# A decoder layer on one core: x and the first weights in one array, two warming products, a last tile of 512, 320 and 192 columns

## The chip, the core and the metric

The kernel runs on one core of a Trainium2 chip. A core has a matrix engine (TensorE, PE in the profile; its weight loads are a row of their own, PEld), a vector engine (VectorE, DVE), an activation engine (ScalarE, ACT), a general engine (GpSimd, POOL) and an engine that only issues transfers (SyncE, SP). Each engine works through its own queue in the order of the program and waits on semaphores for the others. SP and ACT issue the transfers (DMAs) between the chip's main memory and the core's on-chip memory SBUF; products are summed in a second one, PSUM, which the kernel uses as eight banks of 512 fp32 columns.

The metric is the time of one execution on the device in microseconds (us), as the median of several executions.

## What is computed

One layer of a decoder with two parallel mixers over 512 tokens of width 1024, and a gated feed-forward block, all in fp32:

```python
proj = x @ w_in[layer]                     # q, k, v, the SSM's input u (512 columns), gate logits
u = proj[..., 3 * QKV_WIDTH:3 * QKV_WIDTH + SSM_WIDTH]
...
mix_out = mixed.astype(x.dtype) @ w_out[layer]
h = layer_norm(DN_ALPHA * x + mix_out.astype(x.dtype), ln1_g[layer], ln1_b[layer])
ff = (jax.nn.silu(h @ w_ff_gate[layer]) * (h @ w_ff_up[layer])) @ w_ff_down[layer]
x = layer_norm(DN_ALPHA * h + ff.astype(h.dtype), ln2_g[layer], ln2_b[layer])
```

Between the lines shown lie dilated attention in three groups, a state-space model (SSM) on u, and the gates. The change touches how the first product, u, gets its operands, and how the last normalization is reached.

## The kernel before

**Splitting.** The kernel gives TensorE its operands in a rounded form of fp32 (fp32r). To keep fp32 accuracy each operand is split into a high part, which ACT makes with a copy (L181), and a low part, the difference, which DVE makes (L182). Each product is then three: high by high, high by low, low by high (`mm3`, L188 to L190). The cast and the difference of any operand must be done before its products.

**The start.** The first product is u. `xT`, x transposed, lies in main memory as 128 partitions by eight k-slices of 512 tokens; the weights of u lie in two units of four k-slices of 512 columns each. SBUF receives x in tiles big4 and big5 (k 0 to 3, k 4 to 7) and the weights in big0 and big1. The slice k = 0 comes in two halves of 256 columns: SP issues the two of x (L276), ACT the two of the weights (L262). Then DVE clears a small tile `warm` (L263), ACT runs one exponential (L264), and TensorE runs three products of the cleared tile, 384 columns wide and in full fp32 (L267), which serve no result. ACT also issues `small`, 24 KB of SSM parameters (L280). SP goes on with x and weights in turn (L271, L258): k = 1, 2 and 3 singly, then 4 and 5, then 6 and 7, each of x and of the weights on its own, and then the streamed weight units (`raw`, L118) and small constants.

The splits of k = 0 (L479, L480, L321) go by halves: for each half ACT casts x, ACT or DVE casts the weights, DVE makes both differences. The other slices are split whole. Between the slices DVE runs some operations on 128 by 16 tiles from `small` (the queue called late, L78): four after k = 0 and k = 1, ten after each later k.

`u_tiles` (L595) does the products: for k = 0 the first two of four row blocks in two halves of 256 columns, then the other two blocks with 512, then for each k four blocks by three products of 512 columns. Its sums are copied out, and the products of the first v (`pv`) follow; these read x in another order of tokens, from tiles `xt` that ACT copies (L495). The first of them lies in big4 again, the second in big5.

**The end.** The feed-forward block's last product (`down`) sums 22 k-slices for four token tiles t of 128 rows and two halves of 512 columns. Its last four k-slices (NLAST) are done tile by tile, so that the normalization of a tile runs beside the products of the next. A tile's normalization is: DVE adds h to each half and measures it (`bn_stats`, L1267), combines the records (`bn_aggr`, L1268), adds the epsilon (L313); POOL takes the power −1/2 (L1100). `normalize_shared` then spreads the rest: DVE does the first half in two steps (both show as L318); for the second half DVE makes a small operand nm (L318, 128 by 1), ACT scales (L1125), POOL multiplies and adds (L1126, L1127). SP stores both halves (L1232).

The last tile, t = 3, has its sum of the first k-slices and h added early. Its last four k-slices are done in four pieces of 256 columns (`last_quarter`: 12 products, an add L321, a measurement L1259). The first piece is issued inside tile 2's `normalize_shared`, between its first step and nm, so on DVE's queue the order is: first step of tile 2, add and measurement of the piece, nm, second step of tile 2, then the pieces 1 to 3, the combination (L1276), L313, and both halves of the last tile in two steps each. POOL's queue has tile 2's L1126 and L1127 and then the last tile's power. SP and ACT store 64 rows each.

Of the kernel before, what the change touches and what calls it, by code (L numbers as in the profile page):

```python
# [10 lines left out]
F32 = mybir.dt.float32  # L11
# [3 lines left out]
ALU = mybir.AluOpType  # L15

P = 128
S = 512
D = 1024
KT = D // P  # L20
NTT = S // P
# [132 lines left out]
def emit(ctx, tc, i, out):  # L154
# [9 lines left out]
    def bank(n, name):  # L164
        return ps.tile([P, 512], F32, tag=f"b{n}", name=name)
# [13 lines left out]
    def split(hi, lo, src, scale=None):  # L179
        if scale is None:  # L180
            act.copy(hi, src)  # L181
            dve.tensor_tensor(lo, src, hi.bitcast(F32), op=ALU.subtract)  # L182
# [31 lines left out]
    def big(n, name, dt=F32):  # L214
        return pa.tile([P, 2048], dt, tag=f"big{n}", name=name)
# [30 lines left out]

    warm = at.tile([P, 512], F32, tag="un", name="warm", bufs=4)
    wact = sa.tile([P, 1], F32, name="wact")
    xr = [big(4 + j, f"x_raw{j}") for j in range(2)]
    xp = act_pair("x")  # L250
    wu = [big(j, f"wu_raw{j}").rearrange("p (k c) -> p k c", k=4) for j in range(2)]
    wup = [[home(j, f"wu{n}{j}", F32R).rearrange("p (k c) -> p k c", k=4) for j in js] for n, js in (("h", (3, 6)), ("l", (7, "g3")))]
    small = sa.tile([P, 3, NGP], F32, name="small")

    cols256 = [slice(0, 256), slice(256, 512)]

    def load_u(k0, k1, queue):
        queue.dma_start(wu[k0 // 4][:, k0 % 4 : k0 % 4 + k1 - k0],  # L258
                        i["w_in"][k0 // 4].rearrange("p (k c) -> p k c", k=4)[:, k0 % 4 : k0 % 4 + k1 - k0])

    for e in cols256:
        act.dma_start(wu[0][:, 0, e], i["w_in"][0][:, e])  # L262
    dve.memset(warm[:, 0:P], 0.0)  # L263
    act.activation(wact, warm[:, 0:1], AF.Exp)  # L264
    wb_ = dense("warm_b")
    for _ in range(3):
        pe.matmul(wb_[:, 0:384].rearrange("p (n m) -> p n m", n=3), warm[:, 0:P], warm[:, 0:P].unsqueeze(1).broadcast_to([P, 3, P]),  # L267
                  start=True, stop=True)

    def load_x(k0, k1):  # L270
        sp.dma_start(xr[k0 // 4][:, 512 * (k0 % 4) : 512 * (k0 % 4 + k1 - k0)], i["xT"][:, 512 * k0 : 512 * k1])  # L271

    for k0, k1 in ((0, 1), (1, 2), (2, 3), (3, 4), (4, 6), (6, 8)):
        if k0 == 0:
            for e in cols256:
                sp.dma_start(xr[0][:, e], i["xT"][:, e])  # L276
        else:
            load_x(k0, k1)
        if k0 == 0:
            act.dma_start(small, i["ssm_small"])  # L280
        else:
            load_u(k0, k1, sp)
    w.n_dma = 2
    w.n_split = 4
    w.load()
# [34 lines left out]
    def tt(o, a, b, op, eng=dve):  # L320
        eng.tensor_tensor(o, a, b, op=op)  # L321
# [145 lines left out]
            ts(neg[:, n], z, -1.0, ALU.mult, eng=eng)  # L467


    def split_x(k):  # L470
        split(xp[0][k // 4][:, k % 4, :], xp[1][k // 4][:, k % 4, :], xr[k // 4][:, 512 * (k % 4) : 512 * (k % 4) + 512])

    for k in range(KT):
        if k == 0:

            (xh, uh), (xl, ul) = ((z[0][:, 0, :] for z in (xp[n], wup[n])) for n in range(2))
            xs, us = xr[0][:, 0:512], wu[0][:, 0, :]
            for n, c in enumerate(cols256):
                act.copy(xh[:, c], xs[:, c])  # L479
                (act.copy if n else dve.tensor_copy)(uh[:, c], us[:, c])  # L480
                tt(xl[:, c], xs[:, c], xh[:, c].bitcast(F32), ALU.subtract)
                tt(ul[:, c], us[:, c], uh[:, c].bitcast(F32), ALU.subtract)
            late.take(4)
            continue
        split_x(k)
        split(wup[0][k // 4][:, k % 4], wup[1][k // 4][:, k % 4], wu[k // 4][:, k % 4])
        late.take(4 if k < 2 else 10)


# [626 lines left out]
    def normalize_shared(z, mv, ln, between=None):  # L1116

        nm = bt.tile([P, 1], F32, tag="nm", name="nm")
        lo, hi = halves
        norm_first(z, mv, ln, lo)  # L1120
        if between:
            between()
        stt(nm, mv[:, 0:1], -1.0, mv[:, 3:4], ALU.mult, ALU.mult)
        norm_second(z, mv, ln, lo)
        act.activation(z[:, hi], z[:, hi], AF.Identity, bias=nm, scale=mv[:, 3:4])  # L1125
        pool.tensor_tensor(z[:, hi], z[:, hi], ln[:, 0, hi], op=ALU.mult)  # L1126
        pool.tensor_tensor(z[:, hi], z[:, hi], ln[:, 1, hi], op=ALU.add)  # L1127
# [122 lines left out]
    bsts = [bt.tile([P, 4, 6], F32, name=f"bstb{t}", bufs=1) for t in range(NTT)]  # L1250
    mvs = [bt.tile([P, 4], F32, name=f"mvb{t}", bufs=1) for t in range(NTT)]
    quarters = [slice(256 * q, 256 * q + 256) for q in range(4)]

    def last_quarter(q):
        b = bank(4 + q, f"dq{q}")[:, 0:256]
        for k in range(NFF - NLAST, NFF):
            down(b, k, NTT - 1, quarters[q], k == NFF - NLAST, k == NFF - 1)
        tt(end[:, quarters[q]], end[:, quarters[q]], b, ALU.add)
        dve.bn_stats(bsts[NTT - 1][:, q, :], end[:, quarters[q]])  # L1259

    for t in range(NTT - 1):
        z, bst, mv = hn[t], bsts[t], mvs[t]
        for e, cs in enumerate(halves):
            for k in range(NFF - NLAST, NFF):
                down(acc[t][e], k, t, cs, False, k == NFF - 1)
            stt(z[:, cs], z[:, cs], ALPHA, acc[t][e], ALU.mult, ALU.add)
            dve.bn_stats(bst[:, e, :], z[:, cs])  # L1267
        dve.bn_aggr(mv[:, 0:2], bst[:, 0:2])  # L1268
        rstd(mv)
        normalize_shared(z, mv, lnb2, (lambda: last_quarter(0)) if t == NTT - 2 else None)  # L1270
        for cs in halves:
            store((sp, sp), t, z, cs)
    for q in range(1, 4):
        last_quarter(q)
    mv = mvs[NTT - 1]
    dve.bn_aggr(mv[:, 0:2], bsts[NTT - 1])  # L1276
    rstd(mv)
# [29 lines left out]
def layout(a):  # L1307
# [37 lines left out]
    return {  # L1345
        "x": x, "xT": xT, "w_in": np.concatenate(parts), "w_br": np.concatenate([units(a[n][0], 4, 256).reshape(2, 2, P, 1024).transpose(0, 2, 1, 3).reshape(2, P, 2048)
                                for n in ("w_ssm_br", "w_attn_br")]),
        "w_glu": pairs(glu.reshape(512, 1024), 4, 256), "w_out": units(a["w_out"][0], 4, 512)[[0, 2, 1, 3]],
        "w_gu": pairs(gu, 8, P), "w_dn": units(a["w_ff_down"][0], 2, 1024),
# [29 lines left out]
```

## Time and profile before

| | |
|---|---|
| median of three runs | 854.07 us (853.74 to 854.55) |
| the profiled execution | 854.85 us, of which the span of the trace is 853.0 us |
| granted clock of TensorE over the span | 0.998 |
| last product of TensorE begins | 844.80 us |
| last transfers of the result issued from | 848.50 us (ACT) |
| read from main memory, written to it | 84.87 MB, 4.46 MB |

A profile is one execution. Times in it are us from the span's start. Ends of TensorE's products are modelled, so the distance between the starts of two products says more than a product's length. In the rows of a timeline the figures are start, length, engine, line, operation, what is written and read, shape and count; in brackets the idle time of the engine before it and what ended it. "x4" means four records put together. An "issue" row is one of a queue that issues transfers.

### The profile page before, as it was taken

The numbers are of one execution on the slowest core, as the hardware profiler recorded it, in microseconds if no ns is written. First come the engines' busy times: TensorE is split into PE (matmuls) and PEld (weight loads), VectorE is DVE, ScalarE is ACT, GpSimd is POOL, SyncE is SP. The second block draws the span as 40 slices with busy tenths as digits, with TensorE's granted clock in tenths as the row PEclk, the third lists the DMA queues.
The fourth block names the chain that finished last, engine by engine and source line by source line (L and its number), as shares of the span: only waits on it lengthen the run. The fifth ranks groups of instructions, "written<-read, shape, count | busy, mean of one in ns | idle before, by whom it ended". The sixth has DMA issues, their size and how long they took to land.

```text
span 853.0 us, 11310 instructions
## 1 busy us (share of the span) xinstructions
PE 843.6 (99%) x4576; PEld 703.1 (82%) x4576; DVE 485.5 (57%) x949; ACT 303.0 (36%) x481; POOL 25.4 (3%) x27
## 2 busy tenths in 40 slices
PE   9999999999999999999999999999999999999996
PEld 7888888888888888888888898888888888888885
DVE  7976899974666446347785854433434443222237
ACT  7873331164444444643241332222222222211111
POOL 0000000000000000000000500000000000000005
PEclk9999999999999999999999999999999999999999
DMA  9822421425121321121642142222222222322204
GB/s 338 186 103 98 123 99 50 148 72 177 50 100 50 102 95 54 50 88 61 247 145 102 50 148 99 99 98 99 99 100 98 99 91 89 135 92 94 93 0 99
DMA packets 24613, 90.06 MB, mean 106 GB/s; under 512 B 6385, under 2 KB 11249, under 8 KB 15473
## 3 DMA queue, kind: packets, MB, share of 16 engines
q1 hardware_dynamic: 22768, 86.59, 30.1%
q10 hardware_dynamic: 1792, 2.74, 0.9%
q8 instruction: 36, 0.59, 0.3%
q14 instruction: 17, 0.13, 0.0%
HBM read 84.87 MB, written 4.46 MB: 105 GB/s over the span
## 4 chain that ended last, share of the span: by engine, by line
PE 99%; DVE 0%; issue 0%; DVEq 0%
PE fg L189 9%; PE fg L188 9%; PE fg L190 9%; PE dn L188 4%; PE dn L190 4%; PE dn L189 4%; PE pg L188 4%; PE pg L190 3%; PE pg L189 3%; PE pu L595 3%; PE pv L188 3%; PE pk L188 3%; PE pq L188 3%; PE pv L189 3%; PE pq L190 3%; PE pv L190 3%
## 5 line engine op out<-in xcount | busy, mean ns | idle before, releaser
L182 DVE TENSOR_TENSOR wlo<-raw,whi 128x1024 fp32r<-128x1024 f32 x134 | 164.4, 1227 | 193.5 <-ACT whi L181 193.5
L181 ACT CAST whi<-raw 128x1024 fp32r<-128x1024 f32 x134 | 140.1, 1047 | 234.6 <-PE dn L190 73.3
L188 PE MATMUL fg<-hh,whi 128*128 128x512 f32 (+1 forms) x376 | 141.4, 376 | 0.0
L190 PE MATMUL fg<-hh,wlo 128*128 128x512 f32 (+1 forms) x376 | 141.3, 376 | 0.0
L189 PE MATMUL fg<-hl,whi 128*128 128x512 f32 (+1 forms) x376 | 141.3, 376 | 0.0
L188 PEld LDWEIGHTS fg<-hh,whi 128*128 128x128 f32 x376 | 70.8, 188 | 12.9
L190 PEld LDWEIGHTS fg<-hh,wlo 128*128 128x128 f32 x376 | 70.8, 188 | 12.8
L189 PEld LDWEIGHTS fg<-hl,whi 128*128 128x128 f32 x376 | 70.8, 188 | 12.6
L190 PE MATMUL dn<-whi,ff 128*128 128x512 f32 x168 | 65.4, 389 | 0.0
L188 PE MATMUL dn<-whi,ff 128*128 128x512 f32 x168 | 65.4, 389 | 0.0
L189 PE MATMUL dn<-wlo,ff 128*128 128x512 f32 x168 | 65.4, 389 | 0.0
L188 PE MATMUL pg<-x_hi,whi 128*128 128x512 f32 x128 | 50.5, 395 | 0.0
L184 ACT ACTIVATE ff<-fth 128x512 fp32r<-128x512 f32 x22 | 14.0, 634 | 102.7 <-DVE fth L321 102.7
L190 PE MATMUL pg<-x_hi,wlo 128*128 128x512 f32 x128 | 49.9, 390 | 0.0
L189 PE MATMUL pg<-x_lo,whi 128*128 128x512 f32 x128 | 49.9, 390 | 0.0
L321 DVE TENSOR_TENSOR fth<-fth,fg 128x512 f32<-128x512 f32 x22 | 15.1, 688 | 56.9 <-PE fg L190 56.8
L188 PE MATMUL pq<-x_hi,whi 128*128 128x512 f32 x96 | 37.9, 395 | 0.0
L188 PE MATMUL pk<-x_hi,whi 128*128 128x512 f32 x96 | 37.8, 394 | 0.0
L190 PE MATMUL pq<-x_hi,wlo 128*128 128x512 f32 x96 | 37.5, 390 | 0.0
L190 PE MATMUL pk<-x_hi,wlo 128*128 128x512 f32 x96 | 37.4, 390 | 0.0
L189 PE MATMUL pk<-x_lo,whi 128*128 128x512 f32 x96 | 37.4, 390 | 0.0
L189 PE MATMUL pq<-x_lo,whi 128*128 128x512 f32 x96 | 37.4, 390 | 0.0
(256 smaller groups left out, 1463.0 us busy)
## 6 DMA issues: line engine op xcount, KB each, us to landing
raw<-in_w_in SPq DMA_DIRECT2D x26, 1024.0 KB, 4.8
raw<-in_w_gu SPq DMA_DIRECT2D x22, 1024.0 KB, 4.7
raw<-in_w_dn SPq DMA_DIRECT2D x11, 1024.0 KB, 4.7
raw<-in_w_br SPq DMA_DIRECT2D x4, 1024.0 KB, 4.8
raw<-in_w_out SPq DMA_DIRECT2D x4, 1024.0 KB, 4.8
raw<-in_w_glu SPq DMA_DIRECT2D x2, 1024.0 KB, 4.7
xn<-in_x SPq DMA_DIRECT2D x2, 1024.0 KB, 8.0
out_dram<-hn SPq DMA_DIRECT2D x14, 128.0 KB, 2.4
```

Of the source, the lines that this page charges most:

```text
L181: act.copy(hi, src)
L182: dve.tensor_tensor(lo, src, hi.bitcast(F32), op=ALU.subtract)
L184: act.mul(hi, src, scale)
L188: pe.matmul(dst, a[0], b[0], start=first, stop=False)
L189: pe.matmul(dst, a[0], b[1], start=False, stop=False)
L190: pe.matmul(dst, a[1], b[0], start=False, stop=last)
L321: eng.tensor_tensor(o, a, b, op=op)
L595: pe.matmul(bs[e][:, cs], wk[a], xk[b], start=(k + a + b + cs.start == 0), stop=(k == KT - 1 and a == 1))
```

## The change

x and the weights of u lie side by side in one array `xw`: for each k-slice, of 128 partitions by 1024, first two halves of x and then two of the weights; in slice 0 the order is first half of x, first half of weights, second half of x, second half of weights. Four SBUF tiles of 2048 columns (big0, big1, big4, big5) take two slices each. Slice 0 comes in two transfers of 512 columns, the first issued by SP and the second by ACT; ACT issues `small` right behind. SP then issues k = 1, 2, 3 singly and 4 and 5, 6 and 7 together, each with x and weights in one transfer. There are two warming products. The splits are the same ones, on other addresses.

At the end the last tile's pieces have 512, 320 and 192 columns, with three measurement records. The first is still issued inside tile 2's normalization.

```diff
-    xr = [big(4 + j, f"x_raw{j}") for j in range(2)]
+    raws = [big(j, f"raw_x{j}").rearrange("p (k e c) -> p k e c", k=2, e=4) for j in (0, 1, 4, 5)]
     xp = act_pair("x")
-    wu = [big(j, f"wu_raw{j}").rearrange("p (k c) -> p k c", k=4) for j in range(2)]
...
-    def load_u(k0, k1, queue):
-        queue.dma_start(wu[k0 // 4][:, k0 % 4 : k0 % 4 + k1 - k0],
-                        i["w_in"][k0 // 4].rearrange("p (k c) -> p k c", k=4)[:, k0 % 4 : k0 % 4 + k1 - k0])
-
-    for e in cols256:
-        act.dma_start(wu[0][:, 0, e], i["w_in"][0][:, e])
+    def load_xw(queue, k0, k1=None, es=slice(None)):
+        ks = slice(k0 % 2, k0 % 2 + (k1 or k0 + 1) - k0)
+        queue.dma_start(raws[k0 // 2][:, ks, es], i["xw"].rearrange("p (k e c) -> p k e c", k=KT, e=4)[:, k0 : k1 or k0 + 1, es])
+
+    for e, queue in enumerate((sp, act)):
+        load_xw(queue, 0, es=slice(2 * e, 2 * e + 2))
+    act.dma_start(small, i["ssm_small"])
     dve.memset(warm[:, 0:P], 0.0)
     act.activation(wact, warm[:, 0:1], AF.Exp)
     wb_ = dense("warm_b")
-    for _ in range(3):
+    for _ in range(2):
         pe.matmul(wb_[:, 0:384].rearrange("p (n m) -> p n m", n=3), warm[:, 0:P], warm[:, 0:P].unsqueeze(1).broadcast_to([P, 3, P]),
                   start=True, stop=True)
 
-    def load_x(k0, k1):
-        sp.dma_start(xr[k0 // 4][:, 512 * (k0 % 4) : 512 * (k0 % 4 + k1 - k0)], i["xT"][:, 512 * k0 : 512 * k1])
-
-    for k0, k1 in ((0, 1), (1, 2), (2, 3), (3, 4), (4, 6), (6, 8)):
-        if k0 == 0:
-            for e in cols256:
-                sp.dma_start(xr[0][:, e], i["xT"][:, e])
-        else:
-            load_x(k0, k1)
-        if k0 == 0:
-            act.dma_start(small, i["ssm_small"])
-        else:
-            load_u(k0, k1, sp)
+    for k0, k1 in ((1, 2), (2, 3), (3, 4), (4, 6), (6, 8)):
+        load_xw(sp, k0, k1)
...
     for k in range(KT):
+        (xh, uh), (xl, ul) = ((z[k // 4][:, k % 4, :] for z in (xp[n], wup[n])) for n in range(2))
+        raw = raws[k // 2][:, k % 2]
         if k == 0:
...
             for n, c in enumerate(cols256):
-                act.copy(xh[:, c], xs[:, c])
-                (act.copy if n else dve.tensor_copy)(uh[:, c], us[:, c])
-                tt(xl[:, c], xs[:, c], xh[:, c].bitcast(F32), ALU.subtract)
-                tt(ul[:, c], us[:, c], uh[:, c].bitcast(F32), ALU.subtract)
+                xs, us = raw[:, 2 * n], raw[:, 2 * n + 1]
+                act.copy(xh[:, c], xs)
+                (act.copy if n else dve.tensor_copy)(uh[:, c], us)
+                tt(xl[:, c], xs, xh[:, c].bitcast(F32), ALU.subtract)
+                tt(ul[:, c], us, uh[:, c].bitcast(F32), ALU.subtract)
             late.take(4)
             continue
-        split_x(k)
-        split(wup[0][k // 4][:, k % 4], wup[1][k // 4][:, k % 4], wu[k // 4][:, k % 4])
+        for n, (hi, lo) in enumerate(((xh, xl), (uh, ul))):
+            split(hi, lo, raw[:, 2 * n : 2 * n + 2].rearrange("p e c -> p (e c)"))
         late.take(4 if k < 2 else 10)
...
-    quarters = [slice(256 * q, 256 * q + 256) for q in range(4)]
+    parts = [slice(0, 512), slice(512, 832), slice(832, 1024)]
 
-    def last_quarter(q):
-        b = bank(4 + q, f"dq{q}")[:, 0:256]
+    def last_part(q):
+        cs = parts[q]
+        b = bank(4 + q, f"dq{q}")[:, 0 : cs.stop - cs.start]
         for k in range(NFF - NLAST, NFF):
-            down(b, k, NTT - 1, quarters[q], k == NFF - NLAST, k == NFF - 1)
-        tt(end[:, quarters[q]], end[:, quarters[q]], b, ALU.add)
-        dve.bn_stats(bsts[NTT - 1][:, q, :], end[:, quarters[q]])
+            down(b, k, NTT - 1, cs, k == NFF - NLAST, k == NFF - 1)
+        tt(end[:, cs], end[:, cs], b, ALU.add)
+        dve.bn_stats(bsts[NTT - 1][:, q, :], end[:, cs])
...
-        normalize_shared(z, mv, lnb2, (lambda: last_quarter(0)) if t == NTT - 2 else None)
+        normalize_shared(z, mv, lnb2, (lambda: last_part(0)) if t == NTT - 2 else None)
...
-    for q in range(1, 4):
-        last_quarter(q)
+    for q in range(1, 3):
+        last_part(q)
...
-    xT = x.T.reshape(KT, P, S).transpose(1, 0, 2).reshape(P, KT * S)
+    xw = np.stack([x.T.reshape(KT, P, 2, 256), parts[0].reshape(2, P, 4, 512).transpose(0, 2, 1, 3).reshape(KT, P, 2, 256)], 2)
+    xw[0] = xw[0].transpose(0, 2, 1, 3)
+    xw = xw.transpose(1, 0, 2, 3, 4).reshape(P, KT * 1024)
```

More of the change, by code (lines that the diff above doesn't have):

```diff
@@ L467, in step_powers @@
             ts(neg[:, n], z, -1.0, ALU.mult, eng=eng)
-    def split_x(k):
-        split(xp[0][k // 4][:, k % 4, :], xp[1][k // 4][:, k % 4, :], xr[k // 4][:, 512 * (k % 4) : 512 * (k % 4) + 512])
     for k in range(KT):
+        (xh, uh), (xl, ul) = ((z[k // 4][:, k % 4, :] for z in (xp[n], wup[n])) for n in range(2))
+        raw = raws[k // 2][:, k % 2]
         if k == 0:
-            (xh, uh), (xl, ul) = ((z[0][:, 0, :] for z in (xp[n], wup[n])) for n in range(2))
-            xs, us = xr[0][:, 0:512], wu[0][:, 0, :]
             for n, c in enumerate(cols256):
-                act.copy(xh[:, c], xs[:, c])
-                (act.copy if n else dve.tensor_copy)(uh[:, c], us[:, c])
-                tt(xl[:, c], xs[:, c], xh[:, c].bitcast(F32), ALU.subtract)
-                tt(ul[:, c], us[:, c], uh[:, c].bitcast(F32), ALU.subtract)
+                xs, us = raw[:, 2 * n], raw[:, 2 * n + 1]
[3 more added lines that the diff above has]
+                tt(ul[:, c], us, uh[:, c].bitcast(F32), ALU.subtract)
             late.take(4)
             continue
-        split_x(k)
-        split(wup[0][k // 4][:, k % 4], wup[1][k // 4][:, k % 4], wu[k // 4][:, k % 4])
+        for n, (hi, lo) in enumerate(((xh, xl), (uh, ul))):
+            split(hi, lo, raw[:, 2 * n : 2 * n + 2].rearrange("p e c -> p (e c)"))
         late.take(4 if k < 2 else 10)
@@ L1249, in emit @@
         stt(end[:, cs], end[:, cs], ALPHA, acc[NTT - 1][e], ALU.mult, ALU.add)
-    bsts = [bt.tile([P, 4, 6], F32, name=f"bstb{t}", bufs=1) for t in range(NTT)]
+    bsts = [bt.tile([P, 3, 6], F32, name=f"bstb{t}", bufs=1) for t in range(NTT)]
     mvs = [bt.tile([P, 4], F32, name=f"mvb{t}", bufs=1) for t in range(NTT)]
-    quarters = [slice(256 * q, 256 * q + 256) for q in range(4)]
-    def last_quarter(q):
-        b = bank(4 + q, f"dq{q}")[:, 0:256]
+    parts = [slice(0, 512), slice(512, 832), slice(832, 1024)]
+    def last_part(q):
+        cs = parts[q]
+        b = bank(4 + q, f"dq{q}")[:, 0 : cs.stop - cs.start]
         for k in range(NFF - NLAST, NFF):
-            down(b, k, NTT - 1, quarters[q], k == NFF - NLAST, k == NFF - 1)
-        tt(end[:, quarters[q]], end[:, quarters[q]], b, ALU.add)
-        dve.bn_stats(bsts[NTT - 1][:, q, :], end[:, quarters[q]])
+            down(b, k, NTT - 1, cs, k == NFF - NLAST, k == NFF - 1)
+        tt(end[:, cs], end[:, cs], b, ALU.add)
+        dve.bn_stats(bsts[NTT - 1][:, q, :], end[:, cs])
     for t in range(NTT - 1):
@@ L1343, in layout @@
         dm[:, h, :, h] = d[:, :, h].T
-    xT = x.T.reshape(KT, P, S).transpose(1, 0, 2).reshape(P, KT * S)
+    xw = np.stack([x.T.reshape(KT, P, 2, 256), parts[0].reshape(2, P, 4, 512).transpose(0, 2, 1, 3).reshape(KT, P, 2, 256)], 2)
+    xw[0] = xw[0].transpose(0, 2, 1, 3)
+    xw = xw.transpose(1, 0, 2, 3, 4).reshape(P, KT * 1024)
     return {
-        "x": x, "xT": xT, "w_in": np.concatenate(parts), "w_br": np.concatenate([units(a[n][0], 4, 256).reshape(2, 2, P, 1024).transpose(0, 2, 1, 3).reshape(2, P, 2048)
+        "x": x, "xw": xw, "w_in": np.concatenate(parts), "w_br": np.concatenate([units(a[n][0], 4, 256).reshape(2, 2, P, 1024).transpose(0, 2, 1, 3).reshape(2, P, 2048)
                                 for n in ("w_ssm_br", "w_attn_br")]),
```

## The prediction, made before the change was run

> **What bounds the kernel.** Read the page first: its head, its busy shares, its chain of work that ended last.
>
> ```profile
> span 853.0 us, 11310 instructions
> PE 843.6 (99%) x4576; PEld 703.1 (82%) x4576; DVE 485.5 (57%) x949; ACT 303.0 (36%) x481; POOL 25.4 (3%) x27
> PE 99%; DVE 0%; issue 0%; DVEq 0%
> ```
>
> TensorE is busy 843.6 of 853.0 us, and the chain runs through it for 99%. So only three things move the time: when its useful products begin, how fast it then runs, and what follows its last product. The change touches only the first and the last. The timeline of the first 10 us shows the beginning (start, duration, engine, line, operation, count; in brackets the idle time before and what ended it).
>
> ```profile
> 1.05 4.21 PE L267 MATMUL warm_b<-warm 128*128 128x384 f32 x6 [1.05 <-DVE warm L263]
> 3.78 0.34 PEld L267 LDWEIGHTS warm_b<-warm 128*128 128x128 f32 x1 [0.30 <-issue]
> 4.42 0.34 PEld L595 LDWEIGHTS pu<-x_hi,wuh 128*128 128x128 f32 x1 [0.30 <-ACT x_hi L479]
> 5.05 0.34 PEld L595 LDWEIGHTS pu<-x_hi,wuh 128*128 128x128 f32 x1 [0.30 <-issue]
> 6.13 0.54 PEld L595 LDWEIGHTS pu<-x_hi,wuh 128*128 128x128 f32 x2
> 6.56 0.52 PEld L595 LDWEIGHTS pu<-x_lo,wuh 128*128 128x128 f32 x2
> 7.24 0.31 PEld L595 LDWEIGHTS pu<-x_hi,wuh 128*128 128x128 f32 x2
> 8.74 1.07 PE L595 MATMUL pu<-x_hi,wuh 128*128 128x512 f32 x4
> 9.65 1.07 PE L595 MATMUL pu<-x_lo,wuh 128*128 128x512 f32 x4
> 3.37 0.29 DVE L480 CAST wuh<-wu_raw 128x256 fp32r<-128x256 f32 x1 [2.37 <-DMA wu_raw<-in_w_in]
> 3.99 0.41 ACT L479 CAST x_hi<-x_raw 128x256 fp32r<-128x256 f32 x1 [0.38 <-DMA x_raw<-in_xT]
> 6.85 0.62 ACT L181 CAST x_hi<-x_raw 128x512 fp32r<-128x512 f32 x1 [2.15 <-DMA x_raw<-in_xT]
> 7.01 0.17 DVE L78 TENSOR_SCALAR t16s<-small 128x16 f32<-128x16 f32 x1 [1.82 <-DMA small<-in_ssm_small]
> 7.53 0.62 ACT L181 CAST wuh<-wu_raw 128x512 fp32r<-128x512 f32 x1
> ```
>
> Weights for a product are loaded while the one before it runs, so the spacing of weight loads is the spacing of products. The warming products are six records for three calls, one per 0.64 us; the last ends at 5.05, where the first pu product begins. Its operands were ready earlier (casts from 3.37 on): the warming products held TensorE, not the data. Four 256-column loads take 0.86 us before 6.56 (two take 0.43) and 0.68 from 6.56 to 7.24. With 0.213 us each slow and 0.12 fast, the pace doubles at about 7.0. From 8.74 to 9.65 four 512-column products take 0.91, 0.2275 each.
>
> **The start.** One warming call goes: two records, 1.28 us, so TensorE is free at 3.78 instead of 5.05. That pays only if data is there. Four transfers of 128 KB (x and weights, first and second half) become two of 256 KB, one per queue; x and weights of a later k share one transfer; SP issues six transfers instead of twelve before the streamed weights. The DMA section and a view by stretches (length, busy time of PE, PEld, DVE, ACT, POOL, clock, DMA share, GB/s):
>
> ```profile
> x_raw<-in_xT SPq DMA_DIRECT2D x2, 128.0 KB, 2.6
> 2.00:3.50 1.50, 1.50 (x4) 0.87 (x3) 0.13 (x1) 1.46 (x3) 0.00 (x0) 1.00 0.99 327
> 3.50:6.00 2.50, 2.50 (x8) 1.62 (x7) 1.66 (x5) 0.81 (x3) 0.00 (x0) 1.00 0.97 251
> ```
>
> Before, the weights' first half landed at 3.37 (DVE waited for it) and x's second at 3.99 (ACT waited). The DMA engines are full from 2.0 to 3.5 at 327 GB/s: 490 KB, nearly all of the first 512 KB. Now both 256 KB start together and share those engines, so I expect both around when the whole 512 KB had come before: 3.95. The near end is 3.37, when half of the bytes were there; the far end, 4.5, moves the 524 KB at the 251 GB/s of the next stretch (2.1 us from 2.0 on) and adds the 0.4 to 0.5 by which the second half landed after 3.5. I take 3.95: it is the row with the same bytes in the same stretch, and the engines' share of 0.99 leaves no room for less. [...]
>
> After landing, ACT's cast of x takes 0.41 (the 3.99 row) and TensorE follows at about 4.45. The first products of each kind need DVE's work 0.43 and 0.86 later, and DVE's queue (cast 0.29, then three differences of about 0.43) keeps up. So pu begins 0.60 earlier, at half pace until 7.0: 0.30 saved. Ends: 3.37 gives 3.87 and 0.59; 4.5 gives 5.0 and 0.03. Between 3.78 and 4.45 TensorE stands idle, which it never did; its price is a rival below.
>
> What is late next is k = 1. Its products began at 8.74 and would begin near 8.4. They need both casts, the second ending at 7.53 + 0.62 = 8.15, which is early enough by 0.25; x and weights now come as one, though, and the first cast can't run ahead. If that transfer lands at 7.5 instead of about 6.9, the casts end at 8.65 and the 0.30 is gone. `small` is issued earlier on ACT's queue; DVE waited for it until 7.01 with the k = 1 differences queued behind. These are first needed 0.91 after 8.4, so they have about 1 us of cover.
>
> A tile moves: big4 now holds x and weights of k = 4 and 5, so the copy xt into it must wait for DVE's last difference there.
>
> ```profile
> 16.68 2.04 ACT L495 CAST xt<-x_hi 128x1024 fp32r<-128x1024 f32 x1
> 16.82 0.68 DVE L182 TENSOR_TENSOR wulg<-wu_raw,wuh 128x512 fp32r<-128x512 f32 x1
> 27.78 0.39 PE L188 MATMUL pv<-whi,xt 128*128 128x512 f32 x1
> ```
>
> ACT's copy slips by up to 17.50 − 16.68 = 0.82, and the copies and weight splits behind it. Their first reader is at 27.78, so I cost it at nothing; without that cover it is 0.82. Fewer issues on SP and longer rows also cost and bring nothing after the first k, since TensorE has no gap there.
>
> **The end.** The last token tile goes from four pieces of 256 to 512, 320 and 192 columns. The timeline of the end:
>
> ```profile
> 838.94 0.39 PE L190 MATMUL dn<-whi,ff 128*128 128x512 f32 x1
> 839.17 0.28 PE L188 MATMUL dq<-whi,ff 128*128 128x256 f32 x1
> 839.37 0.69 DVE L318 SCALAR_TENSOR_TENSOR hn<-hn,dn 128x512 f32<-128x512 f32 x1 [0.34 <-PE dn L190]
> 840.09 0.69 DVE L1267 BATCH_NORM_STATS2 bstb<-hn 128x6 f32<-128x512 f32 x1
> 840.60 0.28 PE L188 MATMUL dq<-whi,ff 128*128 128x256 f32 x1
> 840.82 0.21 DVE L1268 BATCH_NORM_AGGREGATE mvb<-bstb 128x2 f32<-128x12 f32 x1
> 841.79 0.41 DVE L321 TENSOR_TENSOR hn<-hn,dq 128x256 f32<-128x256 f32 x1
> 842.24 0.43 DVE L1259 BATCH_NORM_STATS2 bstb<-hn 128x6 f32<-128x256 f32 x1
> 842.59 0.14 DVE L318 SCALAR_TENSOR_TENSOR nm<-mvb 128x1 f32<-128x1 f32 x1
> 842.76 0.82 ACT L1125 ACTIVATE hn<-hn,nm,mvb 128x512 f32<-128x512 f32 x1 [4.87 <-DVE nm L318]
> 843.66 1.30 POOL L1126 TENSOR_TENSOR hn<-hn,lnb 128x512 f32<-128x512 f32 x1 [1.37 <-ACT hn L1125]
> 845.03 1.26 POOL L1127 TENSOR_TENSOR hn<-hn,lnb 128x512 f32<-128x512 f32 x1
> 845.12 0.42 DVE L321 TENSOR_TENSOR hn<-hn,dq 128x256 f32<-128x256 f32 x1 [0.15 <-PE dq L190]
> 846.03 0.26 DVE L1276 BATCH_NORM_AGGREGATE mvb<-bstb 128x2 f32<-128x24 f32 x1
> 846.33 0.15 DVE L313 TENSOR_SCALAR mvb<-mvb 128x1 f32<-128x1 f32 x1
> 846.57 0.98 POOL L1100 TENSOR_TENSOR mvb<-mvb,epsb 128x1 f32<-128x1 f32 x1 [0.27 <-DVE mvb L313]
> 847.73 0.74 DVE hn L318
> ```
>
> (The last row is of the chain: start, length, what; the second half of the last normalization.) What the change means to win is on DVE behind the last product: adding and measuring 192 columns instead of 256. From 256 to 512 columns either takes 0.27 more, so 64 fewer save 0.07 each; combining three records instead of four saves some 0.03; DVE was also waiting 0.15 for TensorE. The row of 846.33 comes to about 846.13, then, 0.20 earlier (DVE's order below gives 845.1 for the last add). A 192-column product takes between 0.093 (the line through 0.12 and 0.2275) and 0.12; even at 0.12, DVE is what ends last or within 0.2 of it.
>
> But the first piece stands in the middle of tile 2's normalization, ahead of nm on DVE's queue. It now has twelve products of 0.2275 instead of 0.12: the last starts at 839.17 + 11 × 0.2275 = 841.67, and DVE, 0.43 behind (838.94 to 839.37), adds at 842.10, not 841.79. The measuring follows 0.72 later (839.37 to 840.09) at 842.82. After 256 columns nm followed 0.35 later, so after 512 it follows 0.62 later: 843.44 instead of 842.59. (Behind it a half of a normalization, 0.7, and 320 columns' two steps, 0.52 and 0.42, put the last add at 845.1.) Behind nm wait ACT's half (0.17 later), and two POOL instructions (0.90 after ACT, then 1.37 apart): 843.61, 844.51, 845.88, ending at 847.14. POOL takes its instructions in order, and the next one is the power for the last tile, at 847.22 instead of 846.57. It takes 0.98; DVE's second half begins at about 848.24 instead of 847.73, where DVE's own work had set it. So the end is later by 0.51, although its operand is ready 0.20 earlier. The stores behind it shift alike. Ends of this term: −0.20, should POOL not be in the way, and +0.75, should the late stores of tile 2 also meet the last ones.
>
> **Sum.** −0.30 + 0.51 = +0.21. The profiled execution took 854.85 us, 1.85 around its span of 853.0; that gives 855.06. The median shown is 854.07, 0.78 lower; the same sum on it gives **854.3**. That difference lies between two executions of the same kernel and is no part of the sum.
>
> **Rivals.**
> *The idle gap keeps TensorE slow* (slower than before). Mechanism: the pace doubled 5.95 us after the first product (1.05 to 7.0), all of it unbroken. If the 0.67 us of standstill makes that count start over at 4.45, it doubles at 10.4, and 3.4 more us run at half pace: 1.70 lost. With −0.30 and +0.51 that is 1.91: 856.0. It decides from the point at which a gap spoils the count; the trace has none at the start, so nothing shows that point. [...] Chance 0.13.
> *POOL isn't in the way*: ACT's half or the power slips past, and only the DVE saving is left: −0.30 − 0.20, 853.6. Against it, the rows have POOL in order with 0.28 between 846.29 and 846.57, less than the 0.85 by which nm slips. Chance 0.15.
> *The transfers bring nothing*, the change doing no more than relabel the wait: both halves at 4.5, or k = 1 at 7.5. Then only the end is left: +0.51, 854.6. Against it, the same bytes in fewer issues. Chance 0.20.
> *They come early*: 3.37, saving 0.59: 854.0. Chance 0.10.
> The forecast keeps 0.42.
>
> **Range and chances.** All cases but the gap lie between 853.6 and 854.6. With 0.4 on both sides, for runs that differ (853.74 to 854.55), 853.2 to 855.0; to take in more of the gap's case I go to 855.7. What a measurement can tell from no change is 0.2%, 1.7 us: 852.4 to 855.8. Only the gap gets past the upper bound, and not always: slower 0.10. No sum gets below the lower one: faster 0.02. Same 0.88.
>
> **What would show it.** Right: four warming records; a gap of TensorE before the first pu product, ended by ACT's x_hi, near 4.4; the pace doubling where it did, or at least within 7 us of 1.05; k = 1 near 8.4; nm 4.3 us after the first dq product instead of 3.4; the last power starting right after the second POOL product though its operand is ready about 0.9 earlier; the second half of the last normalization near 9.1 after the first dq product instead of 8.56. Wrong: a pace that doubles past 8 us; ACT waiting for k = 1 past 7.4; a pause on POOL before the last power.

## The result, and the profile after

| | changed | before, on the same chips |
|---|---|---|
| median | 856.19 us (854.63 to 857.05, 22 runs) | 854.33 us (853.60 to 854.85) |
| ratio, with its 95% interval | 1.0021 (1.0014 to 1.0028) | 1 |
| the profiled execution, and its span | 855.93 us, 854.1 us | 854.85 us, 853.0 us |

The kernel became slower by 1.9 us of median, more than the 0.2 forecast, and the median lies above the stated range. The runs also lie farther apart: over 2.4 us instead of 1.25. One of the 22 executions of the kernel before took 4842.52 us; it is left out of the range, and without it the median is 854.31.

First the timeline of the beginning of the changed kernel (start, length, engine, line, operation, written and read, shape, count; in brackets the idle time before and what ended it).

```profile
1.05 2.92 PE L268 MATMUL warm_b<-warm 128*128 128x384 f32 x4 [1.05 <-DVE warm L264]
4.40 0.71 ACT L467 CAST x_hi<-raw_x 128x256 fp32r<-128x256 f32 x2 [1.24 <-DMA raw_x<-in_xw]
4.41 0.29 DVE L468 CAST wuh<-raw_x 128x256 fp32r<-128x256 f32 x1 [3.41 <-DMA raw_x<-in_xw]
4.87 0.80 PE L583 MATMUL pu<-x_hi,wuh 128*128 128x256 f32 x2 [0.89 <-ACT x_hi L467]
5.93 0.62 ACT L181 CAST x_hi<-raw_x 128x512 fp32r<-128x512 f32 x1 [0.50 <-DMA raw_x<-in_xw]
6.99 0.54 PEld L583 LDWEIGHTS pu<-x_hi,wul 128*128 128x128 f32 x2
7.42 0.54 PEld L583 LDWEIGHTS pu<-x_hi,wuh 128*128 128x128 f32 x2
9.33 1.07 PE L583 MATMUL pu<-x_hi,wuh 128*128 128x512 f32 x4
28.37 0.39 PE L188 MATMUL pv<-whi,xt 128*128 128x512 f32 x1
```

The useful products begin at 4.87, 0.18 before those of the kernel before (5.05). Yet k = 1 begins at 9.33 instead of 8.74, 0.59 later, and the first pv product is later by the same 0.59 (28.37 against 27.78). Data doesn't explain it: x and weights of k = 1 land at 5.93, earlier than before (6.85 and later), and TensorE has no idle time after 4.87. It runs at half pace for longer: from 6.99 to 7.42 two 256-column products still take 0.43, 0.21 each, where before the pace had doubled at 7.0. Here it doubles at 8.31: two 512-column products take 0.78 from 7.63 on and 0.46 from 8.41 on.

The view by stretches shows what those 3.41 us before the doubling held, and the stretch before them (start and end, length, busy time and count of PE, PEld, DVE, ACT, POOL, then granted clock, share of the DMA engines, GB/s). First after, then before.

```profile
1.48:4.90 3.42, 2.53 (x5) 0.77 (x4) 0.35 (x2) 1.98 (x4) 0.00 (x0) 1.00 0.88 285
4.90:8.31 3.41, 3.41 (x14) 3.31 (x15) 3.34 (x14) 2.77 (x6) 0.00 (x0) 1.00 1.04 423
2.00:3.50 1.50, 1.50 (x4) 0.52 (x2) 0.00 (x0) 1.15 (x2) 0.00 (x0) 1.00 0.81 236
847.98:849.00 1.02, 0.00 (x0) 0.00 (x0) 1.02 (x3) 0.00 (x0) 0.73 (x1) 0.50 0.08 20
```

```profile
0.17:3.58 3.41, 2.53 (x4) 1.51 (x5) 0.38 (x2) 1.87 (x3) 0.33 (x5) 1.00 0.50 156
3.58:7.00 3.42, 3.42 (x13) 2.62 (x12) 1.58 (x5) 0.89 (x4) 0.00 (x0) 1.00 0.96 269
850.09:851.00 0.91, 0.00 (x0) 0.00 (x0) 0.00 (x0) 0.00 (x0) 0.00 (x0) 0.50 1.04 293
```

The clock column says 1.00 where the products run at half pace at the start, so it can't be used there; at the end it records a fall to 0.50 at 847.98 (before: 850.09). But the trace also records the length of the full-clock stretch up to that fall: 839.679 us here, 843.092 before. They differ by 3.413 us, and are 246 and 247 times that step. So in both profiles full clock begins and ends as if on a grid of 3.413 us. Counting back from the fall gives where it began, 8.31 after and 7.00 before, where the rows show the pace doubling, and, if the grid runs on ahead of that, its points there: 4.90 and 1.48 after; 3.58 and 0.17 before. Before, the step from 0.17 to 3.58 was busy for 2.53 us, 74%, and the clock did not rise at its end; behind the next one, full, it did. After, the step from 1.48 to 4.90 holds the standstill, again 2.53 busy, 74%, and again the clock does not rise; behind the next one it does. (The view lets the last warming product end late, at 3.97; with the 3.78 of the spacing, the step is 68% busy.)

Now the end of the changed kernel in its timeline:

```profile
839.82 0.39 PE L188 MATMUL dq<-whi,ff 128*128 128x512 f32 x1
...
844.07 0.14 DVE L308 SCALAR_TENSOR_TENSOR nm<-mvb 128x1 f32<-128x1 f32 x1
...
845.14 1.27 POOL L1114 TENSOR_TENSOR hn<-hn,lnb 128x512 f32<-128x512 f32 x1 [2.21 <-ACT hn L1113]
846.49 1.26 POOL L1115 TENSOR_TENSOR hn<-hn,lnb 128x512 f32<-128x512 f32 x1
846.87 0.15 DVE L303 TENSOR_SCALAR mvb<-mvb 128x1 f32<-128x1 f32 x1
846.94 3.35 DVE L308 SCALAR_TENSOR_TENSOR hn<-hn,mvb,lnb 128x512 f32<-128x512 f32 x4
847.71 1.00 POOL L1088 TENSOR_TENSOR mvb<-mvb,epsb 128x1 f32<-128x1 f32 x1
849.66 1.39 ACTq L1220 DMA_DIRECT2D out_dram<-hn  x2
```

Read it from the first dq product, 839.82. nm comes 4.25 later (before 3.42). The power's operand is ready at 846.87 + 0.15, but the power stands at 847.71, with no idle time ahead of it, right where POOL's second product ends. The last transfers are issued 9.84 after the first dq product; before it was 848.50 − 839.17 = 9.33. So the end takes 0.51 longer.

The power is late, but it isn't what these 0.51 wait for. It ends at 848.71, and DVE, which has no idle time here, comes to the second half of the normalization only at 848.89. (Where DVE does wait for a power, in b_two_nm_first below, it goes on 0.03 after its end.) What is longer is DVE's own work, the four steps of the last normalization, in the row of 846.94; this is the row of the kernel before:

```profile
846.40 2.73 DVE L318 SCALAR_TENSOR_TENSOR hn<-hn,mvb,lnb 128x512 f32<-128x512 f32 x4
```

They begin 0.11 earlier, counted from the first dq product, and take 3.35 instead of 2.73, 0.62 more: 0.51. All of the 0.62 lies in the first of the four, 1.36 instead of 0.74, which begins while POOL's second product still runs (to 847.75). The seven profiles that have a 512-column piece in front of nm all have this long step (1.36), the seven others (at most 0.75) don't. Why the step is long beside a product on POOL, no run shows; DVE's additions and measurements beside these products keep their length (for 256 columns in the kernel before, 0.42 and 0.43 beside them, 0.41 and 0.43 ahead of them).

The two profiled executions thus differ by 0.59 at the start, 0.06 on the way (dq 0.65 later) and 0.51 at the end: 1.16 until the last transfers, 1.08 in their times. The medians differ by 1.86. The rest must come from executions other than these two, and the grid offers a reason, which is the author's estimate: where its points fall relative to the first product differs. In the fourteen profiles, one of each kernel, the clock rises anywhere between 3.97 and 9.29, although the warming products begin at 1.05 wherever there are any; two executions of one kernel were not compared.

### The profile page after: what moved, and what is told of

It is laid out like the page before. It is cut to its first block, busy times and chain, and to the rows that moved or that the text cites. A ratio compares the mean times of both kernels' runs of the same rounds, so it can differ in the third digit from the quotient of the medians.

```text
span 854.1 us, 11265 instructions
## 1 busy us (share of the span) xinstructions
PE 843.5 (99%) x4562; PEld 702.2 (82%) x4562; DVE 485.6 (57%) x947; ACT 302.7 (35%) x481; POOL 25.4 (3%) x27
## 3 DMA queue, kind: packets, MB, share of 16 engines
HBM read 84.87 MB, written 4.46 MB: 105 GB/s over the span
## 4 chain that ended last, share of the span: by engine, by line
PE 98%; DVE 1%; DMA 0%; issue 0%; DVEq 0%; ACT 0%
PE fg L189 9%; PE fg L190 9%; PE fg L188 9%; PE dn L189 4%; PE dn L188 4%; PE dn L190 4%; PE pg L188 4%; PE pg L190 3%; PE pg L189 3%; PE pu L583 3%; PE pv L188 3%; PE pk L188 3%; PE pq L188 3%; PE pq L190 3%; PE pv L189 3%; PE pv L190 3%
```

## The experiments

Theory: the time is lost at both ends. TensorE's standstill between 3.78 and 4.87 spoils one step of the grid and costs about 1.3 us of median; the 512-column piece costs 0.5. Rivals: the loss is the new transfers'; or the end alone; or the standstill is harmless and the profiles show only chance. All times are medians of eleven runs, with the ratio to the kernel before on the same chip.

| run | what it is | median (range), us | ratio (95%) |
|---|---|---|---|
| b_pieces | before, new pieces | 854.85 (854.32 to 855.64) | 1.0007 (0.9998 to 1.0015) |
| a_quarters | changed, old pieces | 855.67 (853.93 to 856.58) | 1.0012 (1.0003 to 1.0021) |
| a_three | changed, three warming calls | 854.71 (854.43 to 855.07) | 1.0003 (0.9995 to 1.0012) |
| a_three_quarters | both of these | 854.26 (854.12 to 855.16) | 0.9998 (0.9989 to 1.0007) |
| a_none | changed, no warming calls | 856.12 (855.43 to 857.62) | 1.0021 (1.0012 to 1.0030) |
| a_half | changed, two and a half calls | 854.92 (854.24 to 856.92) | 1.0010 (1.0001 to 1.0019) |
| b_two | before, two calls | 854.35 (853.92 to 855.07) | 1.0000 (0.9991 to 1.0009) |
| a_four | changed, k = 0 in four transfers | 855.80 (854.65 to 856.56) | 1.0019 (1.0010 to 1.0027) |
| a_one_queue | changed, k = 0 on SP alone | 855.17 (854.17 to 855.90) | 1.0006 (0.9998 to 1.0015) |
| a_one_queue_quarters | the same, old pieces | 854.93 (853.66 to 855.89) | 1.0003 (0.9994 to 1.0012) |
| b_two_nm_first | before, two calls, new pieces behind tile 2 | 854.25 (853.72 to 855.13) | 0.9999 (0.9990 to 1.0008) |
| a_three_middle | changed, three calls, pieces 256, 512, 256 | 854.17 (853.55 to 854.94) | 0.9999 (0.9990 to 1.0008) |

### Each end by itself

The new pieces in the kernel before:

```diff
-    quarters = [slice(256 * q, 256 * q + 256) for q in range(4)]
+    parts = [slice(0, 512), slice(512, 832), slice(832, 1024)]
...
-    for q in range(1, 4):
-        last_quarter(q)
+    for q in range(1, 3):
+        last_part(q)
```

> The kernel before with only the pieces of 512, 320 and 192 columns. Theory: nm slips by 0.85 us behind the 512-column piece, POOL's two products of tile 2 end after the last tile's power could start, the end is 0.5 later: 854.8. In its trace the power starts within 0.1 of the end of the second POOL product and 7.9 to 8.1 us after the first dq product (7.4 before). Rival (the end gains what its shorter last piece saves): 854.1.

Timeline of this run's end:

```profile
838.44 0.39 PE L188 MATMUL dq<-whi,ff 128*128 128x512 f32 x1
842.69 0.14 DVE L318 SCALAR_TENSOR_TENSOR nm<-mvb 128x1 f32<-128x1 f32 x1
845.11 1.26 POOL L1127 TENSOR_TENSOR hn<-hn,lnb 128x512 f32<-128x512 f32 x1
846.33 1.00 POOL L1100 TENSOR_TENSOR mvb<-mvb,epsb 128x1 f32<-128x1 f32 x1
848.28 1.37 ACTq L1232 DMA_DIRECT2D out_dram<-hn  x2
```

nm 4.25 after the first dq product, the power 7.89, the last transfers 9.84: the same distances as in the changed kernel. The median is 854.85 against 854.34, 0.5 more; its interval alone doesn't exclude nothing, but the rows carry the 0.51.

The old pieces in the changed kernel (the same edit the other way round):

```diff
-    parts = [slice(0, 512), slice(512, 832), slice(832, 1024)]
+    quarters = [slice(256 * q, 256 * q + 256) for q in range(4)]
```

> The changed kernel with the four pieces of 256 columns again. Theory: 0.5 less than the changed kernel, 855.7, the rest of the loss being the start's; the power starts 7.4 us after the first dq product. Rival (the end doesn't matter): 856.2.

The end is back (first dq product 840.36, last transfers 849.69, 9.33 apart), and the loss of the start stays: 855.67 against 854.34, 1.33 more. With the 0.51 of b_pieces that makes 1.84 of the 1.86, but each of the two differences is known to some 0.7 us only, so the close fit is chance.

A third warming call back in the changed kernel:

```diff
-    for _ in range(2):
+    for _ in range(3):
```

> The changed kernel with a third warming product again; nothing else. Gap theory: with two products TensorE stands still from 3.8 to 4.87 us, and in most executions that keeps the slow pace up to 3.4 us longer; the third product fills the gap until 5.05, so the start is that of the kernel before and only the late end (+0.5) is left: about 854.8, and the runs lie within some 1.3 us of each other instead of 2.4. Rival (the late data costs, whatever TensorE does meanwhile): no change, 856.2. Rival (a warming product is pure loss): 0.2 to 0.6 more than 856.2.

The loss of the start is gone, and the runs lie within 0.64 us of each other. The new transfers are still there, so they alone do not cost it.

Both undone together, only array and transfers left:

> The changed kernel with three warming products and the four pieces of 256 columns: what is left of the change is the array and its transfers. Theory (the new transfers cost nothing by themselves, since the warming products run until 5.05 in either kernel): 854.2 to 854.3, as before, the two parts undone adding up (1.5 and 0.5 of the 1.9). Rival (the later landing at 4.2 to 4.4 or the later copies cost something of their own): 854.7 or more.

854.26 against 854.56 of the kernel before: not told apart from it. The transfers alone give or cost nothing that shows here.

### The standstill

The changed kernel without any warming (this leaves out only products whose result is not used):

```diff
-    for _ in range(2):
+    for _ in range(0):
```

> The changed kernel without any warming product. Gap theory (a stretch of about 3.4 us counts as a whole, and the part before the gap and the part behind it together don't fill enough of one): two products in front of a gap are worth nothing in most executions, so taking them away too costs little: 856.2 to 856.5, runs from 855.4 to 857.2, and no run as low as the 854.6 to 855.2 that the changed kernel shows in five of 22. Rival (each warming product brings the fast pace nearer, gap or not): the two missing products cost as much as the third one did, or more: 857.5 or above.

It takes as long as with two calls, 856.12. Two calls ahead of a standstill of 1 us are worth nothing in the median. The view by stretches has, from the first product at 4.72 on, one step that is nearly full, and the clock is up at its end:

```profile
4.53:7.94 3.41, 3.22 (x14) 3.12 (x15) 3.23 (x13) 2.79 (x7) 0.00 (x0) 1.00 1.06 427
```

Half a call more, which shortens the standstill and leaves all else:

```diff
+    pe.matmul(wb_[:, 0:192].rearrange("p (n m) -> p n m", n=3), warm[:, 0:P], warm[:, 0:64].unsqueeze(1).broadcast_to([P, 3, 64]),
+              start=True, stop=True)
```

> The changed kernel with two warming products and a third of half the width (192 columns, 0.64 us at the slow pace), so that TensorE stands still from about 4.4 to 4.87 instead of from 3.8. Theory that a gap counts by its length (the busy share of a stretch of about 3.4 us must be over some 70%): 0.5 us of gap leaves 86%, the start is that of before, 854.7 to 854.9. Rival (any gap starts the count anew): as the changed kernel, 856.2.

Here the first half landed at 4.50, no earlier than in the changed kernel, and the products began at 4.96, later than its 4.87; only the standstill is shorter. All the same the median is only 0.42 above that of the kernel before (854.92 against 854.50), where the changed kernel's is 1.86 above. This speaks against all rivals that put the loss into the transfers or into a late first product. Two of the eleven runs still took 856.9, and the interval of the ratio (1.0001 to 1.0019) overlaps that of the changed kernel; that of a_three (up to 1.0012) doesn't.

How busy must a step be? The view by stretches shows the step with the standstill, which in a_half's profile (first) raised the clock and in a_quarters' (second) didn't:

```profile
3.01:6.43 3.42, 3.08 (x10) 2.15 (x9) 1.79 (x7) 1.58 (x5) 0.00 (x0) 1.00 1.04 409
```

```profile
2.46:5.88 3.42, 2.77 (x8) 1.58 (x7) 1.56 (x5) 1.91 (x6) 0.00 (x0) 1.00 1.01 391
5.88:9.29 3.41, 3.41 (x14) 3.02 (x13) 3.34 (x14) 3.17 (x6) 0.00 (x0) 1.00 1.04 432
```

So 3.08 of 3.42, 90%, was enough, and 2.77, 81%, was not. The ends of products are modelled and lie late here: by the spacing of the weight loads the warming products end at 3.78 and, in a_half, at about 4.42, which gives idle times of 0.54 and 0.85 and shares of 84 and 75%. If the busy share decides, the point lies between these; the runs don't narrow it further. The 70% of the expectation was the author's estimate, and too low: 75% was not enough.

That the grid is one grid all fourteen profiles show. In eleven of them full clock lasts 843.092 us, 247 steps of 3.413, in three (the changed kernel, a_quarters and a_none) 839.679, 246 steps, although it begins anywhere between 3.97 and 9.29.

### Earlier data instead of more warming

Two warming calls with the old transfers:

```diff
-    for _ in range(3):
+    for _ in range(2):
```

> The kernel before with two warming products, its own transfers and end. Gap theory: its data is there at 3.4 to 3.7, so TensorE goes from warming to pu at 3.8 with no gap; 1.28 us of slow products less, worth half: 853.7 (0.6 to 0.7 under before). Rival (two products are too few to bring up the clock, gap or not): 855.5 or more.

A miss. The products begin at 3.80 with no standstill, but TensorE then waits for k = 1, as the timeline of this run shows:

```profile
3.80 0.77 PE L595 MATMUL pu<-x_hi,wuh 128*128 128x256 f32 x2
8.24 1.20 PE L595 MATMUL pu<-x_hi,wuh 128*128 128x512 f32 x4 [0.24 <-ACT wuh L181]
```

With 854.35 against 854.34 nothing is won: in the kernel before the arrival of k = 1 holds the start anyway, as soon as the clock rises early enough. It did even with three calls in b_pieces, where the clock rose at 4.27 and TensorE waited 0.53 for it.

k = 0 in four transfers of 128 KB on two queues:

```diff
-    for e, queue in enumerate((sp, act)):
-        load_xw(queue, 0, es=slice(2 * e, 2 * e + 2))
+    for e in range(2):
+        for n, queue in enumerate((sp, act)):
+            load_xw(queue, 0, es=slice(2 * e + n, 2 * e + n + 1))
```

> The changed kernel with slice k = 0 in four transfers of 128 KB as before, two on each queue, from the new array; two warming products, everything else as changed. Theory (two transfers of 256 KB side by side land together, both late): the first half lands at about 3.4 again instead of 4.4, pu starts at 3.8 without a gap: 854.1 to 854.3 (the early start -0.65, the late end +0.5). Rival (the 512 KB transfers right behind on SP's queue hold up the first ones): landing stays near 4.4 and the time near 856.2.

A miss as well, 855.80, and for the same reason, only larger; its timeline:

```profile
3.56 0.86 ACT L468 CAST x_hi<-raw_x 128x256 fp32r<-128x256 f32 x2
4.04 0.77 PE L584 MATMUL pu<-x_hi,wuh 128*128 128x256 f32 x2
7.75 0.62 ACT L181 CAST x_hi<-raw_x 128x512 fp32r<-128x512 f32 x1 [3.04 <-DMA raw_x<-in_xw]
8.94 1.19 PE L584 MATMUL pu<-x_hi,wuh 128*128 128x512 f32 x4 [1.37 <-ACT wuh L181]
```

The first half lands 0.84 earlier, the standstill is nearly gone, the clock is up at 5.06, and TensorE stands for 1.37 us before k = 1, which lands at 7.75 instead of 5.93.

Both k = 0 transfers on SP's queue, one behind the other:

```diff
-    for e, queue in enumerate((sp, act)):
+    for e, queue in enumerate((sp, sp)):
```

> The changed kernel with both transfers of slice k = 0 on SP's queue, the first half ahead of the second, instead of one on SP's and one on ACT's; all else as changed (two warming products, three pieces). Theory that the two halves land together and late (4.4) because they share the transfer engines from two queues: in one queue the first half is served first and lands at 3.5 to 3.8, the second at about 4.4; pu starts at 4.0 to 4.3, the gap is 0.2 to 0.5 and the slow pace no longer lasts into the next stretch: 854.3 to 854.8, of which 0.5 is the late end. Rival (the rate of the first microsecond and a half is low, 90 to 200 GB/s, because only two transfers have been issued then, not because of sharing): the first half lands at 4.2 or later, and the time stays near 856.

In the timeline of this run ACT's first three casts of x show when the halves of k = 0 and then k = 1 land:

```profile
3.65 0.40 ACT L467 CAST x_hi<-raw_x 128x256 fp32r<-128x256 f32 x1 [0.96 <-DMA raw_x<-in_xw]
4.31 0.41 ACT L467 CAST x_hi<-raw_x 128x256 fp32r<-128x256 f32 x1 [0.26 <-DMA raw_x<-in_xw]
7.28 0.62 ACT L181 CAST x_hi<-raw_x 128x512 fp32r<-128x512 f32 x1 [2.26 <-DMA raw_x<-in_xw]
8.47 1.21 PE L583 MATMUL pu<-x_hi,wuh 128*128 128x512 f32 x4 [0.23 <-ACT wuh L181]
```

Now the halves land one after the other, at 3.65 and 4.31. In the changed kernel they landed close together; its list of DMA issues has, at the end of the rows, the time from the issue, at 0.74 for both, to the landing:

```profile
raw_x<-in_xw SPq DMA_DIRECT2D x1, 256.0 KB, 3.6
raw_x<-in_xw ACTq DMA_DIRECT2D x1, 256.0 KB, 3.8
```

So the first half landed 0.75 later with the two transfers on two queues (4.40) than with both on one (3.65). k = 1 again lands late, at 7.28, and the time, 855.17, is above the 854.3 to 854.8 expected. The same with the old pieces:

> The changed kernel with slice k = 0 on one queue and with four pieces of 256 columns: two warming products, no 512-column piece in front of nm. If the one-queue theory holds and k = 1 lands near 6 as in the changed kernel, both the start (0.3 to 0.6 earlier) and the end (as before) are good: 853.8 to 854.1, under both kernels. Rival: k = 0 lands late or k = 1 becomes the wait (as with the two products in the kernel before, where TensorE waited for k = 1 at 8.2): 854.4 or more.

A miss, 854.93, with a wait of 0.54 for k = 1 in its profile. Each way of getting the first half early was paid for with a late second slice, and none beat the kernel before.

### The order at the end

In the kernel before, with two calls, the first new piece is put behind tile 2's normalization:

```diff
-        normalize_shared(z, mv, lnb2, (lambda: last_quarter(0)) if t == NTT - 2 else None)
+        normalize_shared(z, mv, lnb2)
+        if t == NTT - 2:
+            last_part(0)
```

> The kernel before with its own transfers, two warming products, and pieces of 512, 320 and 192 columns, the first of them behind tile 2's normalization instead of inside it, so that nm doesn't wait for it. Theory: start -0.65 as with two products alone; the end 0.2 to 0.3 earlier than before, since POOL is free in time: 853.4, below both kernels. Rival (DVE, now with nm's wait for POOL ahead of the piece, becomes the bound): end as before or later, 853.7 or more.

The timeline of this run's end:

```profile
838.29 0.39 PE L188 MATMUL dq<-whi,ff 128*128 128x512 f32 x1
841.43 0.16 DVE L318 SCALAR_TENSOR_TENSOR nm<-mvb 128x1 f32<-128x1 f32 x1 [0.44 <-POOL mvb L1100]
845.45 0.15 DVE L313 TENSOR_SCALAR mvb<-mvb 128x1 f32<-128x1 f32 x1
845.68 0.99 POOL L1100 TENSOR_TENSOR mvb<-mvb,epsb 128x1 f32<-128x1 f32 x1 [0.52 <-DVE mvb L313]
847.62 1.38 ACTq L1232 DMA_DIRECT2D out_dram<-hn  x2
```

A miss, 854.25 instead of 853.4. POOL now pauses for 0.52 before the power, so it is out of the way, and the end is back at 9.33. It gets no shorter than that, since DVE stands for 0.44 ahead of nm, waiting for POOL's power of tile 2, and all its later work with it: the operand of the last power stands 7.16 after the first dq product, as in the kernel before. The start was held by k = 1, as in b_two.

Last, small outer pieces and a large middle one, with three warming calls:

```diff
-    for _ in range(2):
+    for _ in range(3):
...
-    parts = [slice(0, 512), slice(512, 832), slice(832, 1024)]
+    parts = [slice(0, 256), slice(256, 768), slice(768, 1024)]
```

> The changed kernel with three warming products and pieces of 256, 512 and 256 columns, so that nm waits behind a short piece again, and the long one lies where only TensorE and DVE are at work. Theory (the late end came from the long piece standing in front of nm, and a short last piece is worth little since 192 columns take 0.111 us a product, hardly less than the 0.12 of 256): POOL is free when the last power's operand is ready, TensorE's pieces take 0.16 us less in all than four of 256, and the end is some 0.2 earlier than before: 9.1 to 9.2 us from the first dq product to ACT's first store against 9.33 before and 9.84 in the changed kernel; 854.0 to 854.1 in all, 0.2 to 0.4 under the kernel before, less than these runs can tell apart. Rival (any piece of 512 columns makes DVE the bound): 9.33 or more from the first dq product, 854.3 or more.

The first dq product stands at 838.44 and the last transfers at 847.60: 9.16, the shortest end of all. nm keeps its place, 3.41 after the first dq product, and one add and one measurement are saved behind it. In time it is 854.17 against 854.29, which can't be told from nothing.

## Why the prediction was wrong

- **TensorE free at 3.78.** Right: four warming records, and a gap that ACT's x_hi ends.
- **Both halves land at 3.95.** They landed at 4.40, inside the ends of 3.37 and 4.5, but 0.45 from the value taken. In the stretch from 2.0 to 3.5 the engines moved 236 GB/s at a share of 0.81, not 327 at 0.99. The row of the kernel before was no floor for two larger transfers. The second landed some 0.2 behind the first. The landings read in the kernel before, 3.37 and 3.99, lie on two queues: 3.37 is a half of the weights, on ACT's queue, 3.99 one of x, on SP's; x's other half was cast from 3.20 on, so x's halves are 0.8 apart or more.
- **The first products at 4.45 and the standstill of 0.67.** 4.87 and, by the spacing, 1.09.
- **"Between 3.78 and 4.45 TensorE stands idle": costed as a rival at 0.13.** This is the step that failed. In the sum the standstill cost nothing and the pace still doubled at 7.0, which made the start 0.30 earlier; in the profile it doubles at 8.31, past the 8 us that the prediction gave as a sign of being wrong, and k = 1 begins 0.59 later. a_half, a_none and a_three show that the standstill, not the transfers, does this; in the median it costs about 1.3 us (a_quarters). The rival's 856.0 is close to 856.19, but its mechanism was not the right one: the count doesn't start over at 4.45 and end at 10.4. In the profile a step of 3.41 us, 74% busy, goes by without a rise, and behind the next one, full, the clock rises. The price is of like size because such a step costs 3.41 us at half pace, 1.7 by estimate; that it came so near the median is luck.
- **What could have been read beforehand.** Only a part. The record of the full-clock stretch was in the trace of before; counted back from the drop it gives 7.00, where the pace doubles. The step takes a second profile, the 839.679 us of the changed kernel beside 843.092; only with it come the points 3.58 and 0.17, and the row of 0.17 to 3.58, 74% busy, as a step that was not enough. The prediction priced the rival by the 5.95 us before the doubling, as a count that began with the first product; no run shows such a count.
- **k = 1 late.** Not in this kernel: it landed at 5.93, earlier than either value of the prediction. TensorE waited for it in the profiles of six variants instead, for 0.23 to 1.37.
- **`small` and the moved xt copy.** Nothing, as costed: `small` was read at 6.20, and pv slipped only with k = 1.
- **The end.** Right up to POOL: nm 4.25 after the first dq product (4.27), POOL's second product ends 7.93 after it (7.97). The 0.51 was right by luck. The sum had DVE wait for the late power; in the trace the power stands 7.89 after the first dq product instead of 8.05, and DVE comes to it 0.18 after its end, held up by its own long first step, which the sum didn't have. Had that step kept its 0.74, the power's end, 8.89 after the first dq product, would have set the second half (8.56 before), and the end would be some 0.35 later, an estimate from these rows. The operand of the power came 0.11 earlier instead of 0.20. The 192-column products follow each other by (845.50 − 844.29)/11 = 0.110 (the first and the last of twelve), between the bounds of 0.093 and 0.12; nothing hung on it.

That executions fall into better and worse ones by the place of the grid, and that this makes the medians differ by 1.86 where the two profiles differ by 1.08, is argued from the grid and the spread. Five of the 22 runs of the changed kernel took 854.63 to 855.53, the others 855.76 and more; none of the five was profiled. Two things bear it out. a_quarters has the same start, and in its profile the clock rose 0.98 later (9.29 against 8.31): its k = 1 began 0.33 later (9.66 against 9.33), although its first product began 0.24 earlier (4.63 against 4.87). And if a step that is 80% busy is enough, which lies between the 75% and the 84%, then with a point of the grid between 3.78 and 4.46 the clock rises at once, since the warming products (1.05 to 3.78) fill 2.73 of the 3.41 us ahead of it. That would be one execution in five (0.68 of 3.41), an estimate that takes the points to fall anywhere alike, and would fit the five of 22.

It also stays open why k = 1 lands at 5.93 behind two 256 KB transfers on two queues but only at 7.1 to 7.75 in the variants whose first half lands early. From 3.5 to 6.0 the engines move 409 GB/s in the one case and 255 in the other, as the view by stretches shows for the changed kernel (first) and a_four (second):

```profile
3.50:6.00 2.50, 1.61 (x6) 1.14 (x6) 1.45 (x5) 1.09 (x4) 0.00 (x0) 1.00 1.05 409
```

```profile
3.50:6.00 2.50, 2.44 (x13) 1.99 (x13) 1.72 (x5) 1.16 (x4) 0.00 (x0) 1.00 0.81 255
```

## What to carry to other kernels

Let warming products reach nearly to the first useful product: here a gap of 1 us behind them made them worth as much as none (856.19 against 856.12), and one of 0.54 left the median only 0.42 above the kernel before, the later end included, so price a shorter warming by the latest arrival that the first data can have. A piece of work put ahead of a small operand on one engine is priced by the queues of the engines behind that operand, here POOL's, and by what will then run beside their later work, here DVE's last normalization; the smaller tail behind it didn't pay it back. Making the first transfer early was worth nothing here while the second slice was late.

## What the runs showed of the hardware

- Full clock of TensorE lasted a whole number of steps of 3.413 us in all fourteen profiles, 246 or 247. Behind a step busy for 84% by the spacing (a_half) it began, behind one busy for 75% (a_quarters) it didn't.
- The clock also fell behind a step that was not empty. In the changed kernel the last one before the drop was 35% busy, and the clock fell at its end; in the kernel before one of 53% kept it, and it fell at the end of the next, empty one. The ends of the other profiles agree: no step busy for 35% or less kept the clock, and none of 53% or more lost it. By stretches, the changed kernel first:

```profile
844.57:847.98 3.41, 1.21 (x11) 1.03 (x10) 3.25 (x8) 0.49 (x1) 2.76 (x3) 1.00 0.34 79
```

```profile
843.27:846.68 3.41, 1.81 (x16) 1.61 (x14) 3.09 (x10) 0.31 (x1) 2.67 (x3) 1.00 0.33 77
846.68:850.09 3.41, 0.00 (x0) 0.00 (x0) 2.45 (x4) 0.00 (x0) 0.87 (x1) 1.00 0.46 105
```

- Two transfers of 256 KB, issued at the same time by two queues, landed 0.2 us apart, 3.6 and 3.8 us after their issue at 0.74; on one queue (a_one_queue) they landed at 3.65 and 4.31.
- A step of DVE on 512 columns (subtract, then multiply by a second array) took 1.36 us instead of 0.74 when it began well before the end of a 512-column product on POOL (0.81 in the changed kernel), in seven of seven profiles.
